# Gate products of token-tile pairs as seven quadrant products, and one ring of buffers

## The chip, the cores and the metric

The kernel runs on one core of one Trainium2 chip. The metric is the device time of a run in microseconds; the median of three runs is given. The profile is that of one execution, taken on the same core.

## The reference

One layer of a hybrid decoder for a prompt of 2048 tokens (16 tiles of 128) and a sample batch of 64 tokens. All is float32.

```
h = rms_norm(x, norm_pre); z = h @ w_in                 # 1024 -> 3584 columns
a_out = silu(sg) * spatial_gating(gelu(su), gelu(sv))   # gMLP half, chunks of 128 tokens
b_out = silu(rg) * group_norm(retention(q, k, v))       # retention half, 4 heads of 128
mix = concatenate([a_out, b_out]) @ w_out               # 1024 -> 1024
x = x + rms_norm(mix, norm_post)
x = x + sigmoid(x @ w_ple_gate) * (p @ w_ple_proj)      # gate 1024 -> 1024, embedding 256 -> 1024
```

The last line is where the change works. The gate is a product of 2048 x 1024 by 1024 x 1024, the embedding one of 2048 x 256 by 256 x 1024.

## The kernel before

Every operand of a product is split into a high part in a rounded float32 type (F32R) and a low part, the rest. A product of a token tile with a weight chunk of 128 x 512 is then three matmuls, high by high, high by low, low by high, each of 128 x 128 stationary (tokens) and 128 x 512 moving (weights). For the sample's 64 tokens the high and the low part lie side by side in one stationary operand, so two matmuls do. Making a split takes a ScalarE copy (L251 for tokens, L214 or L216 for weights) and a VectorE or GpSimd subtraction (L253, L223, L225).

The work is a list of units, one for a token tile in each of five passes: S (gMLP part of the input projection), R twice (two heads each), C1 (output projection, post norm and residual; stores the new x to DRAM as rows, `x2d`, and transposed, `x2T`) and C2 (gate and embedding, the final output). Tile order is 0 to 7, the sample, 8 to 15. A C2 unit has 24 gate matmuls for each of two groups of 512 columns, each followed by 6 matmuls of the embedding.

The class `Stream` writes out the order of all engines by hand. Its clock is a count: one main matmul issued is one count. `st.at(count, fn)` and `st.later(lag, fn)` place work at a count, generators started with `st.start` go on after the counts that they yield. The counts fix the order on each engine's queue, not the time: an engine may run ahead of TensorE as far as its operands and its buffers let it. `fill` places a weight chunk's load `LAG_W` = 14 counts ahead of its high part (L234 to L236). A unit's operands are loaded two units ahead and split one unit ahead. Loads and most stores are on SyncE's queue, in program order; C1's stores of `x2d` and `x2T` are on ScalarE's queue (L823, L826).

Buffers come from several pools: `ring`, 52 buffers of 2 KB per partition for weights; `big`, 10 of 4 KB for token operands, rows and raw loads; `t2` 10 of 2 KB, `t1` 11 of 1 KB, `v2` 8 of 2 KB and `c4` 2 of 4 KB for intermediate values. In PSUM, `zbank` gives one of 4 banks to main products and `sbank` one of 4 to side work. A tile takes any free buffer of its pool; where none is free, the instruction that first writes it waits for the release of an old one.

After a gate group ScalarE takes the tanh of half the product (L838); after the embedding group VectorE makes (tanh + 1) times the embedding (L850), adds half of it to the residual row (L853), and SyncE stores it. In C1 the chain after a unit is a sum of squares on ScalarE (L807), the scale r on GpSimd (L811, L295, L296), the scaled product on VectorE (L818), the addition to the residual on GpSimd (L822), and the block transposition (L180).

## Time and profile before

| what | value |
| --- | --- |
| median of 3 runs | 1147.72 us (1147.21 to 1148.03) |
| span of the profiled execution | 1146.2 us |
| its instructions | 15123 |
| TensorE matmuls, share of span | 5316, 99% |
| VectorE, ScalarE, GpSimd, share of span | 53%, 30%, 38% |
| moved by DMA | 157.75 MB, mean 138 GB/s |

The span runs from the first to the last instruction of one execution. The page lists no other time for that execution; the three runs lie 1.0 to 1.8 us above the span. In the profile PE is TensorE's matmuls and PEld its weight loads, DVE is VectorE, ACT ScalarE, POOL GpSimd and SP SyncE; the engine names with q are their queues. "L196" is line 196 of the kernel, where all matmuls are issued.

### The profile page before, as it was taken

To read this page: it belongs to the slowest core of one execution; us is meant where nothing else is said; L and a number is where in the kernel's file an instruction comes from. 1 tells how busy PE (TensorE), PEld (TensorE's weight loads), DVE (VectorE), ACT (ScalarE), POOL (GpSimd) and SP (SyncE) were. 2 spreads that over 40 slices of the span, in tenths; PEclk is the share of its full clock that TensorE was granted. 3 is DMA by queue.
4 is the path that set the end of the run, shared out by engine and by line. 5 is a ranking of instruction groups with operands and counts; after the bars stand their busy time and mean duration, and the time that the engine had idled before them with its cause. 6 is when DMAs were issued, how large, how long until landed. Compare 5 with 4: busy or idle time off the path is not lost.

```text
span 1146.2 us, 15123 instructions
## 1 busy us (share of the span) xinstructions
PE 1139.0 (99%) x5316; PEld 943.1 (82%) x5316; DVE 604.7 (53%) x1094; ACT 346.5 (30%) x648; POOL 436.3 (38%) x621
## 2 busy tenths in 40 slices
PE   9999999999999999999999999999999999999998
PEld 7888878888888888788888887888888888888886
DVE  4866575566745655675456457643344652233332
ACT  6543433335312322242123123412222421112110
POOL 6654434533334465653444575443334210000000
PEclk9999999999999999999999999999999999999999
DMA  9343123124353442663443427656666763335431
GB/s 312 98 146 96 40 73 119 39 85 135 101 159 96 119 110 81 189 184 97 117 121 95 117 70 213 212 193 191 202 228 227 240 221 120 108 111 150 131 106 55
DMA packets 140300, 157.75 MB, mean 138 GB/s; under 512 B 30656, under 2 KB 106688, under 8 KB 140224
## 3 DMA queue, kind: packets, MB, share of 16 engines
q1 hardware_dynamic: 128336, 139.48, 39.9%
q10 hardware_dynamic: 11888, 17.31, 4.8%
q8 instruction: 42, 0.69, 0.3%
q14 instruction: 34, 0.28, 0.1%
HBM read 110.99 MB, written 45.74 MB: 137 GB/s over the span
## 4 chain that ended last, share of the span: by engine, by line
PE 94%; DMA 2%; POOL 2%; DVE 1%; SPq 1%; issue 0%; ACT 0%; DVEq 0%; ACTq 0%; POOLq 0%
PE z L196 87%; PE s L196 7%; DMA W<-w_in 1%; DMA X<-x 1%; POOL v L377 1%; POOL t L361 0%; SPq L920 0%; DMA X<-sguT 0%; POOL X L253 0%; SPq L207 0%; DVE ti L351 0%; DVE t L337 0%; DVE t L333 0%; DVE W L225 0%; DVE X L305 0%
## 5 line engine op out<-in xcount | busy, mean ns | idle before, releaser
L196 PE MATMUL z<-W,X 128*128 128x512 f32 x4328 | 1072.6, 396 | 1.6 <-DVE W L225 0.8
L196 PEld LDWEIGHTS z<-W,X 128*128 128x128 f32 x4328 | 804.0, 188 | 164.4 <-issue 2.6
L253 DVE TENSOR_TENSOR X<-X,X 128x1024 fp32r<-128x1024 f32 (+1 forms) x68 | 81.1, 1192 | 36.6 <-PE z L196 16.4
L850 DVE SCALAR_TENSOR_TENSOR t<-t,z 128x512 f32<-128x512 f32 (+1 forms) x33 | 22.2, 672 | 142.1 <-PE z L196 142.1
L251 ACT CAST X<-X 128x1024 fp32r<-128x1024 f32 (+1 forms) x82 | 83.7, 1020 | 32.9 <-issue 22.8
L196 PEld LDWEIGHTS s<-t,t 128*128 128x128 f32 (+1 forms) x400 | 73.6, 186 | 13.1 <-issue 3.1
L196 PE MATMUL s<-t,t 128*128 128x128 f32 (+2 forms) x400 | 76.3, 272 | 0.0
L498 ACT ACTIVATE t<-z,rsall 128x256 f32<-128x256 f32 x32 | 15.2, 476 | 196.4 <-PE z L196 191.9
L180 DVE STREAM_TRANSPOSE t<-t 128x256 f32<-128x256 f32 (+3 forms) x69 | 39.8, 577 | 61.5 <-POOL t L478 42.5
L838 ACT ACTIVATE t<-z 128x512 f32<-128x512 f32 x32 | 19.1, 598 | 170.5 <-PE z L196 167.6
L474 POOL TENSOR_TENSOR t<-t,t 128x256 f32<-128x256 f32 (+1 forms) x34 | 27.3, 802 | 100.4 <-DVE t L471 86.3
L225 DVE SCALAR_TENSOR_TENSOR W<-W,c_npre,W 128x512 fp32r<-128x512 f32 x56 | 44.7, 819 | 19.9 <-ACT W L216 19.8
L822 POOL TENSOR_TENSOR X<-X,t 128x512 f32<-128x512 f32 (+1 forms) x34 | 45.7, 1364 | 18.1 <-DVE t L818 12.0
L196 PE MATMUL z<-W,t 128*128 128x512 f32 x200 | 50.9, 389 | 0.0
L535 POOL TENSOR_TENSOR ti<-ti,c_cols 128x2 f32<-128x2 f32 (+1 forms) x34 | 11.2, 328 | 96.1 <-DVE ti L531 96.1
L504 POOL TENSOR_TENSOR t<-t,gnw 128x256 f32<-128x256 f32 (+1 forms) x34 | 40.1, 1178 | 18.8 <-DVE t L502 18.4
L216 ACT ACTIVATE W<-W,c_npre 128x512 fp32r<-128x512 f32 x56 | 39.1, 719 | 25.7 <-DMA W<-w_in 23.4
L807 ACT ACTIVATE t<-z 128x512 f32<-128x512 f32 x32 | 19.1, 598 | 91.1 <-PE z L196 91.1
L196 PEld LDWEIGHTS z<-W,t 128*128 128x128 f32 x200 | 37.5, 188 | 7.8
L529 DVE BATCH_NORM_STATS2 ti<-s 128x6 f32<-128x128 f32 x64 | 15.8, 288 | 50.3 <-PE s L196 50.3
L377 POOL TENSOR_TENSOR v<-t,v 128x128 fp32r<-128x128 f32 x64 | 31.4, 512 | 23.4 <-ACT v L375 17.7
L253 POOL TENSOR_TENSOR X<-X,X 128x1024 fp32r<-128x1024 f32 (+1 forms) x14 | 32.9, 2353 | 15.7 <-ACT X L251 9.6
(118 smaller groups left out, 1042.5 us busy)
## 6 DMA issues: line engine op xcount, KB each, us to landing
X<-xT SPq DMA_DIRECT2D x45, 512.0 KB, 4.0
X<-x SPq DMA_DIRECT2D x32, 512.0 KB, 5.0
W<-w_in SPq DMA_DIRECT2D x56, 256.0 KB, 4.4
qkT<-t SPq DMA_DIRECT2D x132, 64.0 KB, 2.0
x2T<-c ACTq DMA_DIRECT2D x66, 128.0 KB, 2.6
t<-qkT SPq DMA_DIRECT2D x32, 256.0 KB, 3.0
X<-mixT SPq DMA_DIRECT2D x16, 512.0 KB, 4.4
x2d<-X ACTq DMA_DIRECT2D x16, 512.0 KB, 2.7
```

The lines of the kernel that those rows point to most:

```text
L180: V.transpose(out=out.rearrange("p b k r -> p k b r"), in_=src.rearrange("p (k b r) -> p k b r", b=4, r=32))
L196: PE.matmul(out, lhsT=l, rhs=r, start=start, stop=stop)
L216: S.activation(out=hi, in_=raw, func=AF.Copy, scale=sc)
L225: V.scalar_tensor_tensor(out=lo, in0=raw, scalar=sc, in1=f(hi), op0=ALU.mult, op1=ALU.subtract)
L251: S.copy(out=hi, in_=raw)
L253: eng.tensor_tensor(out=lo, in0=raw, in1=f(hi), op=ALU.subtract)
L377: GP.tensor_tensor(out=los[q][:, :, t % 4, :], in0=i, in1=f(o), op=ALU.subtract)
L474: GP.tensor_tensor(out=qk[:, :, 0, :], in0=t1[:, :, 0, :], in1=t2[:, :, 1, :], op=ALU.subtract)
L504: GP.tensor_tensor(out=g, in0=g, in1=ret["gn"][0:n, 256 * pr : 256 * pr + 256], op=ALU.mult)
L807: S.activation(out=junk, in_=src, func=AF.Square, accum_out=acc["a"][:, g : g + 1])
L822: GP.tensor_tensor(out=x2[:, c], in0=x2[:, c], in1=w, op=ALU.add)
L850: V.scalar_tensor_tensor(out=th[g][:, h], in0=th[g][:, h], scalar=1.0, in1=src[:, h], op0=ALU.add, op1=ALU.mult)
```

## The change

The gate is computed for two token tiles (t0, t1) together, by seven products of quadrants in place of eight (the Winograd form of Strassen's method). The two halves of the 1024 features and the two tiles form the quadrants A11 (t0, first half), A12 (t0, second half), A21 and A22 (the same of t1); the weights' quadrants are B11 to B22. GpSimd makes four sums of token quadrants (S1 to S4) and, once, four sums of weight quadrants (T1 to T4); each operand of a product is then split into high and low parts as before. The seven products go to four PSUM banks: m1, u2 and u3 are accumulated one on another in bank a, m5 and c12 in bank c, c21 and c11 have banks of their own. After m1, m5, u2 and u3 ScalarE copies the running sum to a buffer; VectorE adds such copies to the results of c12, u3, c21 and c11, which gives the four gate quadrants. The sample uses four plain quadrant products.

The embedding products of a pair stand between the quadrant products of the next pair, 6 after each of the first four; the last pair has also its own, after u3 and c21.

The pools `ring`, `big`, `v2`, `t2`, `t1` and `c4` become one ring of 101 slots of 2 KB (values of 1 KB take a slot too), with two buffers of 4 KB apart from it for C1's transposition. Tiles of 4 KB become two halves, and so their loads, splits and sums of squares come in halves, in every pass. The residual's store to `x2d` moves from ScalarE's queue to SyncE's. The gate's weights are loaded and prepared in 28 steps from 360 counts ahead of C1's last unit on. The scratch memory for descriptors is set to 1024 bytes.

```diff
+SLOTS = 101
...
-    ring = ctx.enter_context(tc.tile_pool(name="ring", bufs=52))
-    big = ctx.enter_context(tc.tile_pool(name="big", bufs=10))
+    ring = ctx.enter_context(tc.tile_pool(name="ring", bufs=SLOTS))
...
+    def slot(label, shape, dt=F32):
+
+        return ring.tile(shape, dt, tag="slot", name=name(label))
...
-    def vtile(shape, dt=F32):
-        return work.tile(shape, dt, tag="v2", name=name("v2"), bufs=8)
-
-    def xtile(shape, dt=F32):
-        return big.tile(shape, dt, tag="X", name=name("X"))
+        return slot("W", shape, dt)
...
+    def xhalves(shape, dt=F32, label="X"):
+        return [slot(label, shape, dt) for _ in range(2)]
...
     def t2k(shape, dt=F32):
-        return work.tile(shape, dt, tag="t2", name=name("t2"), bufs=10)
+        return slot("t2", shape, dt)
...
     def t1k(shape, dt=F32):
-        return work.tile(shape, dt, tag="t1", name=name("t1"), bufs=11)
...
+    PRODUCTS = {
+        "m1": ("A11", "B11", "a"), "m5": ("S1", "T1", "c"), "u2": ("S2", "T2", "a"), "c12": ("S4", "B22", "c"),
+        "u3": ("S3", "T3", "a"), "c21": ("A22", "T4", "d"), "c11": ("A12", "B21", "b"),
+    }
+    ORDER = ("m1", "m5", "u2", "c12", "u3", "c21", "c11")
+
...
+    def fast_weights(src, scale=None):
...
+        def load(r, c, k):
+            raw = slot("wraw", [P, 512])
+            SY.dma_start(out=raw, in_=src(c, 4 * r + k))
+            raws[r, c, k] = raw
...
+        def job(key, k, raw, needs=(), total=None):
...
+            def high():
+                hi = slot("W", [P, 512], F32R)
+                S.copy(out=hi, in_=raw())
+                cell.append(hi)
...
+            def low():
+                lo = slot("W", [P, 512], F32R)
+                V.tensor_tensor(out=lo, in0=raw(), in1=f(cell[0]), op=ALU.subtract)
+                table[key, k] = (cell[0], lo)
+                cell.clear()
...
+        def combine(dst, x, y, op):
+            GP.tensor_tensor(out=raws[dst], in0=raws[x], in1=raws[y], op=op)
+
+        for k in range(4):
+            job("B11", k, lambda k=k: raws[0, 0, k], [(0, 0, k)])
+        for k in range(4):
+            job("T1", k, lambda k=k: raws[0, 0, k], [(0, 1, k)],
+                lambda k=k: combine((0, 0, k), (0, 1, k), (0, 0, k), ALU.subtract))
+        for k in range(4):
+            job("T2", k, lambda k=k: raws[0, 0, k], [(1, 1, k)],
...
+        for k in range(4):
+            job("B22", k, lambda k=k: raws[1, 1, k])
...
+            job("T3", k, lambda k=k: raws[0, 1, k], [],
+                lambda k=k: combine((0, 1, k), (1, 1, k), (0, 1, k), ALU.subtract))
+        for k in range(4):
+            job("T4", k, lambda k=k: raws[0, 0, k], [(1, 0, k)],
+                lambda k=k: combine((0, 0, k), (1, 0, k), (0, 0, k), ALU.subtract))
+        for k in range(4):
+            job("B21", k, lambda k=k: raws[1, 0, k])
+        return table, jobs
...
+    def fast_fill(jobs, counts):
+        for (loads, scales, total, high, low), c in zip(jobs, counts):
+            for fn in loads:
+                st.at(c - 8 - LAG_W, fn)
+            for fn in scales:
+                st.at(c - 9, fn)
+            if total:
+                st.at(c - 7, total)
+            st.at(c, high)
+            st.at(c + 4, low)
...
+            for i, h in ((0, 0), (0, 1)) if self.sample else ((0, 0), (1, 0), (1, 1), (0, 1)):
+                t = self.tiles[i]
+                raw = slot("X", [P, np_(t) // 32, 4, 32])
+                SY.dma_start(out=raw, in_=self.source[t].rearrange("a p k r -> p a k r")[:, :, 4 * h : 4 * h + 4, :])
+                self.raw[i, h] = raw
...
+                hi, lo = ops = slot("A", [P, 4, P], F32R), slot("A", [P, 4, P], F32R)
...
+            S.copy(out=hi, in_=raw)
+            yield 4
+            V.tensor_tensor(out=lo, in0=raw, in1=f(hi), op=ALU.subtract)
+            self.ops[key] = ops
...
+        def total(self, x, y, op):
+            out = slot("sum", [P, 4, 4, 32])
+            GP.tensor_tensor(out=out, in0=x, in1=y, op=op)
+            return out
...
+            sums = {
+                "S1": lambda: self.total(r[1, 0], r[1, 1], ALU.add),
+                "S2": lambda: self.total(tot["S1"], r[0, 0], ALU.subtract),
+                "S4": lambda: self.total(r[0, 1], tot["S2"], ALU.subtract),
+                "S3": lambda: self.total(r[0, 0], r[1, 0], ALU.subtract),
+            }
+            raw = {"A11": r[0, 0], "A22": r[1, 1], "A12": r[0, 1]}
+            keys = [PRODUCTS[p][0] for p in self.order]
+            todo = [x for x in keys if x in sums]
+            for i, x in enumerate(keys):
+                if todo:
+                    y = todo.pop(0)
+                    tot[y] = sums[y]()
+                yield from self.split(x, tot[x] if x in tot else raw[x])
+                yield 8
...
+                for k in range(4):
...
+                        def go(x=x, y=y, b=b, k=k, j=j, new=new):
+                            self.need(x)
+                            start, stop = k == 0 and j == 0, k == 3 and j == 2
+                            if start and new:
+                                banks[b] = zbank() if b in "ac" else sbank()
+                            hi, lo = self.ops[x]
+                            wh, wl = self.tab[y, k]
+                            mm(banks[b], (hi, hi, lo)[j][:, k, :], (wh, wl, wh)[j], start and new, stop, not new)
+
+                        seq.append((go, None))
+                seq[-1] = (seq[-1][0], lambda p=p: st.start(self.after(p, banks)))
+                if i < len(self.aside):
+                    seq += self.aside[i]
...
+        def after(self, p, banks):
+            t0, t1 = self.tiles
+            c = self.parts = getattr(self, "parts", {})
+            yield 1
+
+            def copy(key, b):
+                c[key] = slot("C", [P, 512])
+                S.copy(out=c[key], in_=banks[b])
+
+            def add(key, b, t, part):
+                V.tensor_tensor(out=c[key], in0=banks[b], in1=c[key], op=ALU.add)
+                st.start(self.post_(t, part, c[key]), 1)
+
+            if p == "m1":
+                copy("m1", "a")
+            elif p == "m5":
+                copy("m5", "c")
+            elif p == "u2":
+                copy("u2", "a")
+            elif p == "c12":
+                add("u2", "c", t0, 1)
+            elif p == "u3":
+                copy("u3", "a")
+                add("m5", "a", t1, 1)
+            elif p == "c21":
+                add("u3", "d", t1, 0)
+            else:
+                add("m1", "b", t0, 0)
...
+        r = tiny(1)[0:n]
+        GP.tensor_tensor(out=r, in0=acc[:, 0:1], in1=acc[:, 1:2], op=ALU.add)
+        rms_scale(r, r, n, 1.0 / D)
+        yield 6
+        x2 = [h[0:n] for h in c1.pop(("tok", t))]
+        for j in range(2):
+            w = t2k([P, 512])[0:n]
+            V.scalar_tensor_tensor(
+                out=w, in0=c1.pop((j, t)), scalar=r, in1=ret["npost"][j][0:n], op0=ALU.mult, op1=ALU.mult
+            )
+            yield 3
+            GP.tensor_tensor(out=x2[j], in0=x2[j], in1=w, op=ALU.add)
+            store(x2d[t][:, 512 * j : 512 * j + 512], x2[j])
+        yield 12
+        bt = blocks(block_rows(n), x2, n)
+        scatter(x2T[t], bt, n, S)
...
+    def c2_begin(tiles):
+        def load():
+            for t in tiles:
+                for g in (1, 0):
+                    tl = slot("x2", [P, 512])[0 : np_(t)]
+                    SY.dma_start(out=tl, in_=x2d[t][:, 512 * g : 512 * g + 512])
+                    c2["x2", t, g] = tl
+
+        st.later(40 if 15 in tiles else 68, load)
...
+    def c2_post(t, g, src):
+        th = src[0 : np_(t)]
+        S.activation(out=th, in_=th, func=AF.Tanh, scale=0.5)
+        c2["th", t, g] = th
+        yield 1
...
+        yield 1
+        th, x2 = c2.pop(("th", t, g)), c2.pop(("x2", t, g))
+        w = 256 if t == 14 and g == 0 else 512
+        for o in range(0, 512, w):
+            h, c = slice(o, o + w), slice(512 * g + o, 512 * g + o + w)
+            V.scalar_tensor_tensor(out=th[:, h], in0=th[:, h], scalar=1.0, in1=ple[:, h], op0=ALU.add, op1=ALU.mult)
+            V.scalar_tensor_tensor(out=x2[:, h], in0=th[:, h], scalar=0.5, in1=x2[:, h], op0=ALU.mult, op1=ALU.add)
+            store((a["o_ys"] if t == SAMPLE else a["o_y"][t])[:, c], x2[:, h])
...
+    unitsC1 = [Unit("C", [t], tabC1) for t in order]
+    unitsC2, before = [], []
+    for j, tiles in enumerate(pairs[:4] + [[SAMPLE]] + pairs[4:]):
+        aside = [ple_products(*tg) for tg in before]
+        if tiles[0] == SAMPLE:
+            before = [(SAMPLE, 1), (SAMPLE, 0)]
+        else:
+            t0, t1 = tiles
+            before = [(t0, 1), (t1, 1), (t1, 0), (t0, 0)]
+        if j == 8:
+            own = [ple_products(*tg) for tg in before]
+            aside = (aside + [[]] * 4)[0:4] + [own[0], own[1] + own[2] + own[3]]
+        unitsC2.append(Fast(tiles, tabC2, x2T, c2_post, c2_begin, aside, c2_operands))
...
-        for steps, us in ((stepsR[1], unitsR[0]), (stepsC1, unitsR[1])):
-            fill(steps, first8(us[-3]) + [begin[us[-1]] + 6 + 6 * j for j in range(8)])
-        fill(stepsC2, [begin[unitsC1[-7]] + 40 * j for j in range(8)] + [begin[unitsC1[-1]] + c for c in (6, 12, *range(18, 66, 6), 70, 76)])
+        us = unitsR[0]
+        fill(stepsR[1], first8(us[-3]) + [begin[us[-1]] + 6 + 6 * j for j in range(8)])
+        us = unitsR[1]
+        fill(stepsC1, first8(us[-3]) + [begin[us[-1]] + 6 + 6 * j for j in range(8)])
+        last = begin[unitsC1[-1]]
+        fast_fill(jobsC2, [last - 20 * (18 - j) for j in range(18)] + [last + 8 + 9 * j for j in range(10)])
+        fill(stepsP, [last + 90 + 10 * j for j in range(4)])
...
+            if isinstance(u, Fast):
+                lead = 92, 54
...
+            st.at(begin[u] - lead[0], u.load)
+            st.at(begin[u] - lead[1], lambda u=u: start_prep(u))
...
+    nc = bacc.Bacc("TRN2", target_bir_lowering=False, num_devices=1, dynamic_dma_scratch_size=1024)
```

## Rows read from the trace of the kernel before

**Rows 1.** The page, its head and part 1: busy us of each engine.

```profile
span 1146.2 us, 15123 instructions
...
PE 1139.0 (99%) x5316; PEld 943.1 (82%) x5316; DVE 604.7 (53%) x1094; ACT 346.5 (30%) x648; POOL 436.3 (38%) x621
```

**Rows 2.** The page, part 4: chain that ended last, shares by engine.

```profile
PE 94%; DMA 2%; POOL 2%; DVE 1%; SPq 1%; issue 0%; ACT 0%; DVEq 0%; ACTq 0%; POOLq 0%
```

**Rows 3.** TensorE's waits, whole span: us in total, times, longest.

```profile
PE s L912 <- POOL zero L162: 1.0, 1, 1.0
PE z L196 <- DVE W L225: 0.8, 2, 0.5
PE z L196 <- ACT W L216: 0.5, 1, 0.5
PE z L196 <- POOL X L923: 0.3, 1, 0.3
```

**Rows 4.** Windows of C1 and C2: engines' busy us, clock, DMA share, GB/s.

```profile
734.00:914.80 180.80, 180.80 (x813) 150.13 (x811) 79.90 (x101) 49.49 (x103) 65.38 (x89) 1.00 0.65 207
914.80:1141.50 226.70, 226.70 (x1001) 187.56 (x999) 77.19 (x111) 45.23 (x77) 3.85 (x5) 1.00 0.40 129
```

**Rows 5.** Timeline of TensorE at the start of C2: start, duration.

```profile
914.80 5.60 PE L196 MATMUL z<-W,X 128*128 128x512 f32 x24
920.24 1.52 PE L196 MATMUL z<-W,t 128*128 128x512 f32 x6
921.60 5.60 PE L196 MATMUL z<-W,X 128*128 128x512 f32 x24
...
928.40 5.60 PE L196 MATMUL z<-W,X 128*128 128x512 f32 x24
```

**Rows 6.** Timeline of all engines at the end.

```profile
1140.11 1.52 PE L196 MATMUL z<-W,t 128*128 128x512 f32 x6
1140.30 0.60 ACT L838 ACTIVATE t<-z 128x512 f32<-128x512 f32 x1 [6.20 <-PE z L196]
1141.73 0.42 DVE L850 SCALAR_TENSOR_TENSOR t<-t,z 128x256 f32<-128x256 f32 x1 [5.38 <-PE z L196]
...
1142.98 0.42 DVE L853 SCALAR_TENSOR_TENSOR X<-t,X 128x256 f32<-128x256 f32 x1
```

**Rows 7.** Groups of instructions in C2: busy us, mean ns, idle before.

```profile
L850 DVE SCALAR_TENSOR_TENSOR t<-t,z 128x512 f32<-128x512 f32 x31 | 21.3, 689 | 136.7 <-PE z L196 136.7
L838 ACT ACTIVATE t<-z 128x512 f32<-128x512 f32 x32 | 19.1, 598 | 170.5 <-PE z L196 167.6 <-DMA x2T<-c 2.9
...
L223 DVE TENSOR_TENSOR W<-W,W 128x512 fp32r<-128x512 f32 x6 | 4.1, 680 | 2.3 <-ACT W L214 2.3
```

**Rows 8.** Timeline of all engines after a unit of C1.

```profile
860.59 0.38 SPq L720 DMA_DIRECT2D X<-mixT  x1
860.60 0.60 ACT L807 ACTIVATE t<-z 128x512 f32<-128x512 f32 x1 [1.68 <-PE z L196]
...
863.48 2.99 POOL L822 TENSOR_TENSOR X<-X,t 128x512 f32<-128x512 f32 x2 [0.87 <-DVE t L818]
...
866.51 1.25 DVE L180 STREAM_TRANSPOSE c<-X 128x1024 f32<-128x1024 f32 x1 [1.18 <-POOL X L822]
```

**Rows 9.** Groups of VectorE, ScalarE and GpSimd in C1, asked by engine.

```profile
L223 DVE TENSOR_TENSOR W<-W,W 128x512 fp32r<-128x512 f32 x12 | 11.0, 923 | 1.7 <-ACT W L214 1.7
...
L214 ACT CAST W<-W 128x512 fp32r<-128x512 f32 x13 | 7.8, 616 | 4.1 <-DMA W<-w_gate 1.8 <-POOL X L822 1.7 <-PE z L196 0.6
...
L822 POOL TENSOR_TENSOR X<-X,t 128x512 f32<-128x512 f32 x30 | 39.8, 1348 | 14.8 <-DVE t L818 9.6 <-issue 5.2
```

**Rows 10.** DMA issues in C1: count, KB each, median us to landing.

```profile
X<-mixT SPq DMA_DIRECT2D x12, 512.0 KB, 4.3
W<-w_gate SPq DMA_DIRECT2D x16, 256.0 KB, 4.3
```

**Rows 11.** Waits of SyncE's queue in C1: us in total, times, longest.

```profile
SPq L720 <- PE z L196: 74.8, 11, 10.1
```

More of the change, by code (lines that the diff above doesn't have):

```diff
@@ new lines, in hybrid_step, with c2_operands @@
+    c2 = {}
+    def c2_begin(tiles):
[6 more added lines that the diff above has]
+        st.later(40 if 15 in tiles else 68, load)
+    def c2_operands(tiles):
+        raws = []
+        for t in tiles:
+            raw = t1k([P, 2, P])[:, :, 0 : np_(t)]
+            SY.dma_start(out=raw, in_=(a["psT"] if t == SAMPLE else a["pT"][t]))
+            raws.append(raw)
+        yield 14
+        for t, raw in zip(tiles, raws):
+            z = slot("A", [P, 2, 2, P], F32R)
+            if t == SAMPLE:
+                hi, lo, ops = z[:, 0, :, 0:TS], z[:, 0, :, TS:P], (z[:, 0],)
+            else:
+                hi, lo = ops = z[:, 0], z[:, 1]
+            S.copy(out=hi, in_=raw)
+            yield 3
+            V.tensor_tensor(out=lo, in0=raw, in1=f(hi), op=ALU.subtract)
+            yield 3
+            c2["p", t] = ops
@@ new lines, in load @@
+                if self.kind == "C":
+                    self.raw[t] = xhalves([P, np_(t) // 32, 4, 32])
+                    for h in range(2):
+                        src = mixT[t].rearrange("a p k r -> p a k r")[:, :, 4 * h : 4 * h + 4, :]
+                        SY.dma_start(out=self.raw[t][h], in_=src)
+                    continue
+                self.raw[t] = load_xT(t)
+                if self.kind == "R":
+                    if t == SAMPLE:
+                        st.start(r_sample_state(self.pr))
+                    cs = work.tile([P, P], F32, tag="cs", name=name("cs"), bufs=3)
+                    SY.dma_start(out=cs[0 : np_(t)], in_=a["cs"][t, 0 : np_(t)])
+                    ret["cs", t] = cs
+                else:
+                    self.raw["tok", t] = load_tok(t)
@@ L752, in begin @@
-        def begin(self):
-            t = self.tiles[0]
-            if self.kind == "C1":
-                self.raw["tok", t] = load_tok(t)
-            elif self.kind == "C2":
-                x2 = xtile([P, D])[0 : np_(t)]
-                SY.dma_start(out=x2, in_=x2d[t])
-                self.raw["x2", t] = x2
+                self.ops[t] = yield from split_cols(self.raw.pop(t), t, GP if self.kind == "S" else V)
+                if self.kind == "S":
+                    yield 2
+                    yield from rms_of_x(t, self.raw["tok", t])
+                    if t == SAMPLE:
+                        st.start(sgu_weights_sample())
@@ L761, in main, with load @@
+        def begin(self):
+            if self.kind == "C":
+                t = self.tiles[0]
+                def load():
+                    c1["tok", t] = load_tok(t)
+                st.later(20, load)
         def main(self):
@@ L791, in main @@
                                 seq += p[3 * k : 3 * k + 3]
-            elif kind == "R":
+            elif kind == "C":
+                t = self.tiles[0]
+                for g in range(2):
+                    seq += group(t, opsof(t), g, range(KD), lambda b, g=g: c1_post(t, g, b))
+            else:
                 t, pr = self.tiles[0], self.pr
@@ L870, in hybrid_step @@
     order = list(range(8)) + [SAMPLE] + list(range(8, NT))
+    pairs = [[2 * j, 2 * j + 1] for j in range(NT // 2)]
     tabS, fillS = weight_pass(in_specs([1, 0, 2]))
```

407 lines of the change are left out of this document (223 added, 184 removed).

## The prediction, made before the changed kernel ran

> **What bounds the kernel now.** I read the page from the top. TensorE is busy for 1139.0 of 1146.2 us [rows 1] and the chain that ended last lies on it for 94% of the span [rows 2]. Busy alone proves little, so the next view is TensorE's own waits: apart from 1.0 us at the very start there are 1.6 us of them in all [rows 3]. Then I cut the span at the change. In the output-projection pass (C1) and the gate pass (C2) the granted clock is 1.00, the 2.4 GHz level, TensorE never stands, VectorE is busy for 80 of 181 and 77 of 227 us, ScalarE for 49 and 45, GpSimd for 65 and 4, and the DMA engines are at 65% and 40% [rows 4]. Last comes the spacing. In C2 a period of 24 gate products and 6 embedding products begins at 914.80 us and the next but one at 928.40: 60 products in 13.60 us, 226.7 ns each, whichever kind they are [rows 5]. C2 has 16 x 60 + 40 = 1000; 1000 x 0.2267 = 226.7 us, from 914.80 to about 1141.5. So C2 costs its count of products times one step, and a product less is worth 0.2267 us for as long as TensorE is still fed.
>
> **What is removed.** A pair of token tiles takes 2 x 48 = 96 gate products now. Seven quadrant products of 4 k-blocks and 3 hi/lo terms are 84. The sample stays at 32 and the embedding at 200. The new C2 has 8 x 84 + 32 + 200 = 904, which is 96 fewer: 96 x 0.2267 = 21.8 us. Shapes are unchanged, so I keep the step. The Trainium skill (TensorE: Matmul & The Clock Gate, "Wait — 56ns, not 53.3ns?") measures 215.7 ns from one product of 512 columns to the next at the full clock; by that page the 96 would bring 20.7 us, an estimate, and the row of this kernel is 5% longer.
>
> **What is added at the end.** Today TensorE ends on embedding products. The tanh of their gate ran beside them (1140.30), and four VectorE instructions of 0.42 us follow from 1141.73 [rows 6]. After the change the product c11 comes last. Behind it stand a VectorE add out of PSUM (priced like L850, 0.69), a tanh (L838, 0.60) [rows 7], two hand-overs between engines, and then the same four instructions. A hand-over took 0.04 us (866.47 to 866.51) [rows 8]; I take 0.1 each. The end grows by 0.69 + 0.60 + 0.2 = 1.5 us; the bounds are 0, if the stores get shorter by as much, and 2.
>
> **What is added beside TensorE in C2.** A full pair is 84 + 24 products, 24.5 us. ScalarE: 7 casts and 4 copies at 0.62, 4 tanh at 0.60, 9.2 us. VectorE: 7 low parts at 0.68 (L223 with GpSimd idle) to 0.92 (with GpSimd at work), 4 adds and 8 instructions of the tail's kind at 0.69 (L850): 13.0 to 14.7 us. GpSimd: 4 sums at 1.35 (L822), 5.4 us [rows 7, 9]. The embedding's own splits are as now. At most 60% of a pair is taken, and all of it is hidden behind 24.5 us of products; without that cover VectorE's 14.7 us would be what a pair costs.
>
> **A new wait.** Banks a and c are read in the middle of a sum: u2 goes on in bank a only when m1 is copied out, c12 in bank c when m5 is, u3 in bank a when u2 is. From the last product of one to the next write of its bank lie 24 products where the embedding stands between (5.4 us), 12 in the first pair, which has none (2.7 us). The copy takes 0.6, so ScalarE may come 4.8 us late, or 2.1 in the first pair, before TensorE stands. In front of it are casts that wait for loads or sums. Quadrants are loaded 92 - 54 = 38 counts (8.6 us) ahead of their first cast and land in some 4.3 us [rows 10]; a sum is asked for a whole product ahead. In the first pair there are also weight steps of T4 and B21: from load to combination 15 counts, 3.4 us, against 4.3 to land, so 0.9 late; the combination takes 1.35 of the 1.6 us that it has; the cast, and what is queued behind it, comes 0.7 us late. That is under 2.1. I take 0; from above three waits of 2 us, 6 us.
>
> **In C1.** Eighteen weight steps stand ahead of the last unit where 8 were: 10 x 0.62 us more on ScalarE, 10 x 0.92 on VectorE and some ten combinations x 1.35 on GpSimd [rows 9], over 181 us with room for each [rows 4]. A unit's two banks are read for the last time some 62 counts after its first product and wanted again at 96, so the chain L807, r, L818 may slip by 34 counts, 7.7 us; a combination and a late cast in front of it are 2 to 3 us. SyncE issues about 7 loads and stores per unit for 3, at 0.38 us each [rows 8], 2.7 of 10.9 us. The residual's two stores move to it from ScalarE's queue, and operand and weight loads stand behind them. They wait for L822, whose second sum ends 5.9 us (26 counts) after its unit's products [rows 8], and are placed 27 and 30 counts after: they hold the queue for little. Loads in halves shorten the runs of the transposed operands. If those 8.4 MB per pass took twice the time, the DMA share would go from 65% to 79% in C1 and from 40% of 227 us to 57% of 205 in C2, worked out from the rates in [rows 4]: still hidden. S and R keep their products; a lag in their added halves would have to use up a whole unit (5 us and more) to show.
>
> **The ring.** One ring of 101 slots serves what five kinds of buffer did. By the lags in the diff, C2 holds 64 slots of weights, up to 12 of operands, 5 quadrants, 2 sums, 5 partial products, 6 residual halves and 4 embedding operands; they do not peak together, and I count 94 at most. Tightest is the point 28 counts ahead of C1's last unit: 32 + 34 weights, 10 raw chunks, 4 quadrants, 8 operands, 8 others, 96. Five are to spare. Today's kernel shows what a full pool does: SyncE stood 74.8 us in all for buffers that TensorE was still reading, up to 10.1 at a time [rows 11], and TensorE waited for none of it [rows 3].
>
> **Sum.** -21.8 + 1.5 = -20.3 us on a span of 1146.2: 1125.9. The median of the runs, 1147.72, stands 1.5 us above that span. Forecast: 1127.5 us, itself between 1124.8 (no growth at the end and 1 of the 1.6 us of early waits gone, as early loads no longer wait for large buffers: 1147.7 - 21.8 - 1.0 = 1124.9) and 1129 (1.5 us of the first pair's bound).
>
> **Rivals.**
> A, stalls at the edges: the first pair's copies, or C1's banks behind late combinations, hold TensorE for 2 to 8 us. For it: only 2.1 us of room, and weight steps that come late already. Against: loads and casts are queued ahead of TensorE and run when they can, not when their count comes. 1129.5 to 1135.5 us. Chance 0.22.
> B, slower: each copy of a partial product needs a fresh slot. If the ring is dry in the steady state, ScalarE stands at the copy until an older slot is free, and TensorE stands with it, three times in each of 8 pairs. That eats the gain when each bank is 20.3 / 24 = 0.85 us late, the copy done 6.3 us behind its product instead of within 5.4. At 2 us each the time is 1127.5 + 48 = 1175. For it: some seven slots to spare by my count in C2. Against: with a slot freed every few products a wait would be short. Chance 0.07, and 0.03 that it stops within 2.3 us of the old time.
> C, C2 does not shorten with its products: the weight loads are busy for 82% of the span [rows 1], and if that were the measure, TensorE would not be the limit. The 226.7 us would stay and the end would grow: 1149. Against: no wait in C2, and a period that repeats to 0.01 us. Chance 0.02. The Trainium skill (Trainium Kernel Development and Optimization, "Performance Expectations") calls matmul busy time a bad metric and weight-load busy a good one; this trace bears it out only as far as that 82%.
>
> **How the numbers follow.** Forecast 0.66, A 0.22, B 0.07 + 0.03, C 0.02. Faster by over 0.2% (2.3 us, about what a measurement of this kernel can tell from no change): 0.66 + 0.22 = 0.88. Within it: 0.03 + 0.02 = 0.05. Slower: 0.07. The range, 1124.8 to 1135.5, takes in the forecast and A.
>
> **What would show it.** Right: C2 in 205 us, still 226.7 ns a product, TensorE waiting for no copy; the last store issued some 1.5 us later after the last product than now. Wrong: TensorE standing at the start of u2, c12 or u3; ScalarE standing at a copy or cast for an old slot; a clock below the 2.4 GHz level in C2; another step; a C1 longer than 181 us.

## The result, and the profile of the changed kernel

The changed kernel takes 1132.4 us (median of four runs: 1131.08, 1133.74, 1130.59, 1133.72), the kernel before 1147.87 on the same chip. The ratio is 0.9865, with an interval of 0.9851 to 0.9879: faster by 15.5 us, inside the predicted range and 4.9 us above the forecast. The profiled execution is the run of 1131.08; its span is 1129.3.

The page, part 1, against [rows 1]:

```profile
PE 1118.1 (99%) x5220; PEld 925.4 (82%) x5220; DVE 687.1 (61%) x1283; ACT 395.7 (35%) x834; POOL 504.8 (45%) x700
```

96 products fewer and TensorE's share as before. VectorE has 82 us more work, GpSimd 69, ScalarE 49. The page can't say where a few us are missing; TensorE's waits over the whole span can, against [rows 3]:

```profile
PE z L202 <- ACT C L907: 1.4, 1, 1.4
PE s L202 <- DVE W L229: 1.4, 2, 0.9
PE s L1209 <- POOL zero L163: 1.0, 1, 1.0
PE s L202 <- ACT W L220: 0.4, 1, 0.4
```

L907 is the copy of a partial product, L220 and L229 are the high and low parts of the embedding's weights. These three waits are new. The same view has three more, 0.9 us in all, ahead of C1. The timeline of TensorE puts them at two places, the start of u2 in the first pair and the first six embedding products that stand in the second pair:

```profile
912.68 6.51 PE L202 MATMUL z<-W,A 128*128 128x512 f32 x28
920.63 8.46 PE L202 MATMUL z<-W,A 128*128 128x512 f32 x36 [1.45 <-ACT C L907]
928.93 5.60 PE L202 MATMUL s<-W,A 128*128 128x512 f32 x24
934.37 2.88 PE L202 MATMUL z<-W,A 128*128 128x512 f32 x12
937.35 0.50 PE L202 MATMUL s<-W,A 128*128 128x512 f32 x1
938.35 0.73 PE L202 MATMUL s<-W,A 128*128 128x512 f32 x2 [0.51 <-DVE W L229]
939.44 0.50 PE L202 MATMUL s<-W,A 128*128 128x512 f32 x1 [0.36 <-ACT W L220]
940.85 0.73 PE L202 MATMUL s<-W,A 128*128 128x512 f32 x2 [0.91 <-DVE W L229]
```

From 934.37, 18 products should take 4.1 us; the next group of 12 begins at 941.42, 7.05 later. So 3.0 us go here. That is more than the 1.8 that the waits hold, because a product that stands alone takes 0.50 us in these rows and not the step of 0.2267. Another 1.6 go at 920.63 (28 products from 912.68 should end their steps at 919.03), together 4.6. After that nothing is lost. A later pair in the same view:

```profile
961.84 2.88 PE L202 MATMUL z<-W,A 128*128 128x512 f32 x12
...
986.32 0.84 PE L202 MATMUL z<-W,A 128*128 128x512 f32 x3
```

From 961.84 to 986.32 are 24.48 us for 108 products, 226.7 ns each, as in [rows 5]. What the other engines do at the two places is seen by windows (busy us of each engine, granted clock, DMA share, GB/s), the first the whole of C1, against [rows 4]:

```profile
734.00:913.70 179.70, 179.70 (x806) 149.13 (x805) 93.22 (x136) 55.37 (x126) 91.44 (x106) 1.00 0.67 208
```

and the change from C1 to C2 in steps of 10 us:

```profile
895.00:905.00 10.00, 10.00 (x46) 8.28 (x45) 5.81 (x8) 3.54 (x8) 9.14 (x9) 1.00 0.66 192
905.00:915.00 10.00, 10.00 (x46) 8.29 (x45) 6.40 (x8) 3.60 (x7) 10.00 (x8) 1.00 0.64 215
915.00:925.00 10.00, 8.55 (x38) 6.78 (x37) 10.00 (x11) 7.74 (x15) 8.89 (x9) 1.00 0.54 150
925.00:935.00 10.00, 10.00 (x46) 8.29 (x45) 9.93 (x12) 2.33 (x5) 6.75 (x5) 1.00 0.86 277
```

The columns after the length are TensorE's products, its weight loads, VectorE, ScalarE, GpSimd. GpSimd is half busy over C1 (91 of 180 us) and all but full at its end (9.14 and 10.0 of 10 us); then VectorE is full for 20 us. How the one leads to the other shows in the timeline of these two and ScalarE:

```profile
907.80 1.74 POOL L835 TENSOR_TENSOR sum<-X,sum 128x512 f32<-128x512 f32 x1
908.31 1.78 DVE L830 TENSOR_TENSOR A<-sum,A 128x512 fp32r<-128x512 f32 x1
909.50 1.73 POOL L994 TENSOR_TENSOR X<-X,t 128x512 f32<-128x512 f32 x1
911.19 2.54 POOL L765 TENSOR_TENSOR wraw<-wraw,wraw 128x512 f32<-128x512 f32 x2
912.51 0.62 ACT L753 CAST W<-wraw 128x512 fp32r<-128x512 f32 x1 [3.48 <-POOL wraw L765]
913.16 1.12 DVE L758 TENSOR_TENSOR W<-wraw,W 128x512 fp32r<-128x512 f32 x1 [3.08 <-ACT W L753]
...
915.94 0.62 ACT L828 CAST A<-sum 128x512 fp32r<-128x512 f32 x1 [1.55 <-DVE bt L184]
...
920.00 0.58 ACT L907 COPY C<-z 128x512 f32<-128x512 f32 x1
...
934.63 0.63 ACT L1035 ACTIVATE C<-C 128x512 f32<-128x512 f32 x1 [4.28 <-DVE C L910]
935.17 0.60 ACT L220 CAST W<-W 128x512 fp32r<-128x512 f32 x1
```

ScalarE stands 3.48 us at a weight cast for a weight sum (L765), which stands behind a token sum (L835) and a residual add (L994) on GpSimd. VectorE stands behind that cast, 3.08 us. When both go on, VectorE is late with some ten subtractions, and many of them are long: up to 1.78 us beside a GpSimd sum, against 0.69 on average for the same instruction in four later pairs. The copy at 920.00 waits for nothing when its turn comes. It is late because ScalarE's queue ahead of it stood for the weight sum and then another 1.55 us, at a store that waits for VectorE's transposition. The second stall comes the same way: the casts of the embedding's weights (L220) stand behind a tanh that waits 4.28 us for an add of VectorE (L910).

The end, in the timeline of all engines, against [rows 6]; the last product ends at about 1123.4 and the span at 1129.3, 5.9 us after it, where it was 4.6 (1141.6 and 1146.2):

```profile
1120.73 2.65 PE L202 MATMUL s<-W,A 128*128 128x512 f32 x11
...
1123.43 0.69 DVE L910 TENSOR_TENSOR C<-s,C 128x512 f32<-128x512 f32 x1 [2.60 <-PE s L202]
1124.15 0.63 ACT L1035 ACTIVATE C<-C 128x512 f32<-128x512 f32 x1 [6.17 <-DVE C L910]
1124.81 0.42 DVE L1049 SCALAR_TENSOR_TENSOR C<-C,s 128x256 f32<-128x256 f32 x1 [0.69 <-ACT C L1035]
```

The group of 28 at 912.68 holds C1's last 4 products, so C2 starts at 913.6, 1.2 us earlier than in [rows 4]. The account of the span: -21.8 for the products, -1.2 for the start, +4.6 for the two stalls, +1.3 for the end, -17.1; measured 1146.2 - 1129.3 = 16.9.

### The profile page after: what moved, and what is told of

Its sections match the earlier page's. It is cut to its first block, busy times and chain, and to the rows that moved or that the text cites. A ratio compares the mean times of both kernels' runs of the same rounds, so it can differ in the third digit from the quotient of the medians.

```text
span 1129.3 us, 15843 instructions
## 1 busy us (share of the span) xinstructions
PE 1118.1 (99%) x5220; PEld 925.4 (82%) x5220; DVE 687.1 (61%) x1283; ACT 395.7 (35%) x834; POOL 504.8 (45%) x700
## 4 chain that ended last, share of the span: by engine, by line
PE 95%; DVE 1%; POOL 1%; issue 1%; DMA 1%; ACT 0%; SPq 0%; DVEq 0%; ACTq 0%; POOLq 0%
PE z L202 80%; PE s L202 16%; POOL wraw L765 1%; DVE W L758 0%; DVE A L830 0%; DMA t<-xT 0%; POOL sum L835 0%; POOL X L994 0%; DVE C L910 0%; DMA wraw<-w_gate 0%; DVE W L229 0%; ACT A L828 0%; POOL A L1221 0%; ACT C L1035 0%; DVE x L1050 0%
## 5 line engine op out<-in xcount | busy, mean ns | idle before, releaser
L202 PE MATMUL z<-W,A 128*128 128x512 f32 x4040 | 1007.5, 396 | 2.4 <-ACT C L907 1.4
L202 PEld LDWEIGHTS z<-W,A 128*128 128x128 f32 x4040 | 750.1, 188 | 153.3 <-issue 2.6
L202 PE MATMUL s<-W,A 128*128 128x512 f32 x464 | 112.5, 390 | 1.9 <-DVE W L229 1.4
L202 PEld LDWEIGHTS s<-W,A 128*128 128x128 f32 x464 | 86.9, 188 | 21.2 <-DVE W L229 2.0
L262 DVE TENSOR_TENSOR A<-X,A 128x512 fp32r<-128x512 f32 (+1 forms) x102 | 73.4, 722 | 46.1 <-ACT A L260 39.3
L260 ACT CAST A<-X 128x512 fp32r<-128x512 f32 (+1 forms) x130 | 78.2, 603 | 22.8 <-issue 14.6
L835 POOL TENSOR_TENSOR sum<-X,X 128x512 f32<-128x512 f32 x16 | 23.1, 1445 | 93.1 <-DMA X<-x2T 44.8
L994 POOL TENSOR_TENSOR X<-X,t 128x512 f32<-128x512 f32 (+1 forms) x34 | 46.3, 1382 | 14.0 <-DVE t L990 13.0
L1035 ACT ACTIVATE C<-C 128x512 f32<-128x512 f32 (+1 forms) x34 | 21.5, 632 | 63.2 <-DVE C L910 60.9
L262 POOL TENSOR_TENSOR A<-X,A 128x512 fp32r<-128x512 f32 (+1 forms) x28 | 35.5, 1273 | 14.3 <-ACT A L260 14.3
L347 ACT ACTIVATE t<-z,rsall 128x512 f32<-128x512 f32 x29 | 19.8, 687 | 60.9 <-PE z L202 60.8
```

Source lines behind the costliest of these rows:

```text
L202: PE.matmul(out, lhsT=l, rhs=r, start=start, stop=stop, skip_group_check=again)
L260: S.copy(out=hi, in_=r)
L262: eng.tensor_tensor(out=lo, in0=r, in1=f(hi), op=ALU.subtract)
L347: S.activation(out=g, in_=src, func=AF.Square, scale=rs)
L835: GP.tensor_tensor(out=out, in0=x, in1=y, op=op)
L994: GP.tensor_tensor(out=x2[j], in0=x2[j], in1=w, op=ALU.add)
```

## The experiments

The main question was where 4.6 us of the gain went, and why; the rest tests the prediction's other terms. Unless said otherwise an edit is made to the changed kernel, and its time is to be held against 1132.4 and 0.9865 [0.9851, 0.9879].

**The embedding products of the first pair later.** They stand after c12, u3, c21 and c11 of the second pair, and no longer after its first four products.

```diff
+        if j == 1:
+            aside = [[], [], []] + aside
         unitsC2.append(Fast(tiles, tabC2, x2T, c2_post, c2_begin, aside, c2_operands))
```

> The embedding products of the first pair, which stand in the second pair, are moved three products later (after c12, u3, c21 and c11 instead of m1, m5, u2 and c12). Theory 1, VectorE has a backlog of some 10 us at the change from C1 to C2 and the embedding's weight parts stand in it: the broken stretch of 6 embedding products (937.1 to 941.4 us, 3.0 us longer than six steps) is whole again, the span falls by 2.7 to 3.0 us, to about 1126.4, and the runs that showed a granted clock of 0.997 or 0.998 instead of 0.999 no longer do, so that the median falls by more, to 1128. Rival, all that VectorE makes is late: the wait moves to the operands of m5, u2 or c12 of the second pair and the time stays within 0.5 us of the changed kernel's.

1135.49 us, 0.9892 [0.9879, 0.9906], 3 us slower. TensorE's waits:

```profile
PE z L202 <- ACT C L907: 5.9, 2, 4.4
```

and its timeline at the second pair:

```profile
939.82 0.39 PE L202 MATMUL z<-W,A 128*128 128x512 f32 x1
944.64 7.36 PE L202 MATMUL z<-W,A 128*128 128x512 f32 x24 [4.43 <-ACT C L907]
```

The wait for embedding weights is gone and a larger one for the copy stands in front of u2 of the second pair. So it is not those weights alone that are late, but what ScalarE and VectorE make as a whole. The edit has two other effects. The embedding products are also the 6 x 0.2267 us of room that a copy has, and here that room is gone. And the granted clock falls behind the longer stall: the 24 products take 7.36 us, for 5.60 at the 2.4 GHz level, so 1.8 us of what this execution loses are the clock.

**The end covered.** The last pair's second half of embedding products is put behind c11.

```diff
-            aside = (aside + [[]] * 4)[0:4] + [own[0], own[1] + own[2] + own[3]]
+            aside = (aside + [[]] * 4)[0:4] + [own[0], own[1] + own[2], own[3]]
```

> Of the last pair's own embedding products the last six stand behind c11, not before it. Theory 1 (the end grew because an add of 0.69 and a tanh of 0.63 us stand behind the last product): those 1.4 us run beside six products of 1.36 us, and the span falls by 1.2 to 1.3 us. Rival, the end grew for another reason, its stores or queues: no change.

1130.92 us, 0.9857 [0.9843, 0.9870]. The timeline at the end: c11's add runs beside six products that end at about 1125.0, the span ends at 1129.5, 4.5 later, where it was 4.6 before the change.

```profile
1119.81 5.15 PE L202 MATMUL s<-W,A 128*128 128x512 f32 x22
...
1123.64 0.69 DVE L910 TENSOR_TENSOR C<-s,C 128x512 f32<-128x512 f32 x1 [1.23 <-PE s L202]
```

The 1.3 us at the end are shown by the trace; the intervals of the two times overlap, so the time alone would not show them. Nor does the span, 1129.5 for 1129.3: in this execution the granted clock fell after the second stall (0.83 in 935 to 945 us), which it did not in the changed kernel's.

**No weight sums.** GpSimd's sums T1 to T4 are left out, so the gate is computed with the plain weight chunks in their place; everything else runs.

```diff
-            if total:
-                st.at(c - 7, total)
```

> GpSimd's 16 subtractions that make T1 to T4 are left out, so the gate is computed from the plain quadrants and its values are not the reference's. All other instructions stay. Theory 1 as a question of speed, GpSimd at work on SBUF stretches VectorE's subtractions: the low parts of the gate's weights fall from 1.08 us on average to below 0.8, the backlog shrinks, and of the 4.6 us that TensorE loses in the first two pairs at least 3 come back: a span of 1126.3 or less. Rival, the sheer number of VectorE's instructions there makes the backlog: the low parts may get faster but TensorE still loses 3.5 us or more. Second rival, slots of the ring: no change, as no slot is freed earlier.

1127.15 us, 0.9821 [0.9808, 0.9835], 5.2 us faster, and the four runs lie within 0.3 us. The profiled executions, in neither of which the clock fell in C2, lie 4.1 us apart (1125.2 and 1129.3), which is the stalls; the rest goes with the clock, told below. Of TensorE's waits in C2 one is left:

```profile
PE s L202 <- DVE W L229: 0.4, 1, 0.4
```

and the window shows GpSimd with time to spare:

```profile
905.00:915.00 10.00, 10.00 (x46) 8.29 (x45) 9.56 (x12) 4.41 (x10) 7.27 (x5) 1.00 0.60 206
```

GpSimd's weight sums are what the stalls hang on. VectorE does more of its work ahead of C2 (9.56 of 10 us in 905 to 915, for 6.40). That its subtractions would then get short was a miss: L758 still takes 987 ns on average over the pass, for 1078, and between 895 and 941 us, where the stalls were, nearly as long as before:

```profile
L758 DVE TENSOR_TENSOR W<-wraw,W 128x512 fp32r<-128x512 f32 x11 | 13.4, 1225 | 0.4 <-ACT W L753 0.3
```

**The ring alone.** The ring, the halves and the queues of the new kernel with the old gate, tile by tile, in it.

```diff
-    unitsC2, before = [], []
...
+    unitsC2 = [Unit("G", [t], tabC2) for t in order]
```

> The one ring and the halves stay, but the gate is computed as before, tile by tile with 96 products a pair, its embedding behind each group, 20 weight steps at their old places. Theory: the ring brings the 1.2 us by which R and C2 begin earlier, and nothing else: 1146.7 us, TensorE's waits after the start under 1.5 us. Rival 1, halves and the shared ring cost something in S, R or C1 that the earlier start hides: above 1147.9. Rival 2, the earlier start comes from the changed order of loads near C2 and not from the ring: 1147.9.

1146.96 us (11 runs) for 1147.58 of before (15 runs), 0.9995 [0.9986, 1.0004]. The medians lie 0.6 us apart and the interval reaches from 1.6 us less to 0.5 more, so no cost and no gain of the ring with its halves is shown. Its C1 waits for nothing and C2 begins at 914.2.

**Sums that nobody reads.** GpSimd makes the weight sums into a buffer of their own and the casts take the plain chunks, so the gate's values differ as above: its work stays, the waiting of the casts for it goes.

```diff
-            GP.tensor_tensor(out=raws[dst], in0=raws[x], in1=raws[y], op=op)
+            GP.tensor_tensor(out=slot("unused", [P, 512]), in0=raws[x], in1=raws[y], op=op)
```

> GpSimd makes its 16 weight sums at the same places and speed, but into buffers that nobody reads; T1 to T4 are the plain quadrants, so the gate's values are not the reference's. This separates two ways in which leaving the sums out took 4 us off. Theory A, the casts of T1 to T4 on ScalarE wait for late sums, hold ScalarE's queue and let VectorE's work pile up behind: without the wait the pile is gone, 1127 to 1128 us, TensorE losing under 1 us in the first two pairs. Theory B, GpSimd at work stretches VectorE's instructions and its own residual additions come late behind the sums: the load is the same, so the time stays at 1131 us or more.

1134.53 us, 0.9887 [0.9872, 0.9902], no gain at all; TensorE's three waits in C2 come to 4.6 us, for 3.2. The buffers of the unused sums take slots of the ring, but GpSimd waits for none of them, only for loads. My first theory, that the casts wait for weight sums and hold up what is behind them, falls in this form. The timeline of ScalarE shows what takes their place:

```profile
917.70 0.62 ACT L828 CAST A<-sum 128x512 fp32r<-128x512 f32 x1 [5.74 <-POOL sum L835]
```

The token sums of the first pair stand in the same queue on GpSimd. It is GpSimd's load in this stretch that counts, whoever waits for it first. Whether it counts by its lateness or by what it does to VectorE's subtractions, this run can't tell: both are still there.

**Weights k-block by k-block.** All seven steps of a k-block follow each other, 21 of 28 before C1's last unit, so that sums and plain steps alternate.

```diff
         for k in range(4):
             job("B11", k, lambda k=k: raws[0, 0, k], [(0, 0, k)])
-        for k in range(4):
             job("T1", k, lambda k=k: raws[0, 0, k], [(0, 1, k)],
...
-        for k in range(4):
...
-        fast_fill(jobsC2, [last - 20 * (18 - j) for j in range(18)] + [last + 8 + 9 * j for j in range(10)])
+        fast_fill(jobsC2, [last - 20 * (21 - j) for j in range(21)] + [last + 13 * j for j in range(7)])
```

> The 28 weight steps come k-block by k-block: all seven operands of k = 0, 1 and 2 ahead of C1's last unit, 20 counts apart, and the seven of k = 3 in the order of their products, 13 counts apart, from that unit's start. Raw chunks are free after their k-block, so the ring has room for 21 early steps where there were 18. Seven weight sums of GpSimd between 897 and 919 us become four or five. Theory (GpSimd, fully busy from 895 to 921 us, is what holds the others): TensorE's lost 4.6 us fall below 1.5, the granted clock is 0.999 in all runs, 1127.5 to 1129 us. Rival, VectorE's amount of work at the edge: 3 low parts fewer are 2 to 3 us of its backlog of 10, the loss stays above 3 us, 1130 or more.

1130.91 us, 0.9855 [0.9841, 0.9868], where I had expected 1127.5 to 1129. TensorE waits 2.4 us for a copy and 0.9 for L229, 3.3 together, for 3.2 in the changed kernel. The profiled executions have the same span, 1129.3, so no stall is mended: the median is 1.5 us lower because no run is as long as the two at 1133.7, and the intervals overlap. Of ScalarE's waits between 890 and 945 us one is new in size:

```profile
ACT W L753 <- PE z L202: 3.0, 1, 3.0
```

GpSimd has gaps now (4.45 of 10 us in 895 to 905), but ScalarE stands 3.0 us for a slot of the ring that TensorE still reads, and 8.5 us for weight sums, more than the 6.3 of the changed kernel. Earlier steps need slots that aren't there at that moment.

**Ninety slots.** `SLOTS = 90` for 101.

> The changed kernel with 90 slots in the ring for 101. Theory, the ring is no cause of what TensorE loses: by the count of the prediction up to 96 are in use at one place, so loads there come some counts later, but the time stays within 1 us of the changed kernel's 1130.6 to 1133.7. Rival (the prediction's B): the ring is nearly dry already, and eleven slots less cost 5 us or more, with TensorE waiting at banks a and c in many pairs.

1139.8 us, 0.9932 [0.9920, 0.9945]; I had expected less than 1 us, and it is 7.4. Waits of TensorE in the whole span:

```profile
PE z L202 <- ACT C L907: 8.0, 1, 8.0
PE z L202 <- DVE t L990: 2.0, 1, 2.0
```

Between 890 and 945 us ScalarE stands 11.7 us for slots that TensorE still reads and 9.9 for weight sums. The ring is short at the change from C1 to C2 and nowhere else: the steady pairs show no wait. The 8 us are one wait, in the first pair. Behind it the granted clock is 0.52 in 925 to 935 us, so a part of the 7.4 is the clock.

**Both edits together**, the weights by k-block and the covered end:

> The weight steps by k-block together with the last six embedding products behind c11. If both causes are what the theory says, their gains add: 1.2 us less than the run with the weight steps alone, 1126.3 to 1127.8 us. Rival: the end's gain is taken by something else, and the two runs are equal.

1129.8 us, 0.9846 [0.9833, 0.9859], 1.1 less than the first alone, near the 1.2 expected, though the intervals overlap and the time is above the 1126.3 to 1127.8 expected. By its median it is the fastest version that computes the whole layer, 1.5% under the kernel before.

**103 slots.** `SLOTS = 103`.

> The ring has 103 slots for 101, nothing else. With 101 slots the trace of the changed kernel shows one wait of ScalarE for a slot that TensorE still reads, 1.9 us. Theory (the stalls come from GpSimd's full stretch; 101 slots are enough): 1131.5 to 1133, and TensorE's idle before the copy of L907 stays at 1.2 to 1.6 us, that before the embedding weights at about 1.8. Rival (the ring at 101 still holds the casts up, a milder form of what 90 slots did): the wait for the slot is gone and the time falls by 1 to 3 us, to 1129 to 1131.

1133.14 us, 0.9875 [0.9858, 0.9891]. ScalarE's wait for a slot is gone, TensorE waits 2.6 us for the copy, for 1.45, and 0.9 for the embedding's weights, for 1.8; the time is no better. At 101 the ring is not what binds.

**Six sums on VectorE.** Meant were the last six weight sums; the condition as written fits two others, of T1, some 20 of the 28 steps before the last.

```diff
-            GP.tensor_tensor(out=raws[dst], in0=raws[x], in1=raws[y], op=op)
+            late = y[0:2] == (1, 0) or (x[0:2] == (0, 1) and y[2] > 1)
+            (V if late else GP).tensor_tensor(out=raws[dst], in0=raws[x], in1=raws[y], op=op)
```

> The last six weight sums (T3 from its third k-block, T4) go to VectorE, the other sums stay on GpSimd. GpSimd is relieved of 6 sums of about 1.3 us in 900 to 925 us, VectorE gets 6 of about 0.7 us, 4 us, while it is busy for 6.4 of 10 us in 905 to 915 and without a gap after that. Theory (GpSimd's queue is what is late; token sums stand behind weight sums): the wait for the copy of L907 goes from 1.45 to under 0.5, and the time to 1128 to 1130. Rival (VectorE is as full as GpSimd from 915 us on, so that the work only changes its place): the wait moves to the embedding weights' low parts of L229 and grows there to 3 us or more; 1131 to 1134.

1132.3 us, 0.9865 [0.9850, 0.9880]: as without the edit. It says nothing on the question; moving the late sums to VectorE was not tried. Its trace is of use below, as the changed kernel's own with another clock.

**The transposed tile's stores on SyncE.**

```diff
-        scatter(x2T[t], bt, n, S)
+        scatter(x2T[t], bt, n, SY)
```

> The four stores of each transposed token tile (x2T) are issued from SyncE and not from ScalarE, in all 17 units of C1. ScalarE no longer waits for the transposition of L184 (1.55 us at 915.94 in the changed kernel's trace) with the copies of m1 and m5 behind it. Theory (the first copy is late because of what stands ahead of it on ScalarE, the sums of GpSimd and this store): half of it goes, the wait of 1.45 falls to under 0.6, time 1130.5 to 1132. Rival (the cast ahead of it is late from GpSimd's sums alone, and SyncE's queue now holds quadrant and weight loads behind the transposition): no gain, 1132 to 1136.

1132.73 us, 0.9868 [0.9854, 0.9883], no gain; TensorE waits 2.6 us for the copy, for 1.45. ScalarE no longer waits for the transposition and waits 10.3 us for weight sums in place of 6.3: the rival. With another wait taken out of ScalarE's queue, GpSimd's lateness is what is left.

**T3 before B22, and the covered end.** The steps with four sums change places with four that have none, T4 and B21 come later.

```diff
+        if scale is None:
+            jobs[12:20] = jobs[16:20] + jobs[12:16]
         return table, jobs
...
-        fast_fill(jobsC2, [last - 20 * (18 - j) for j in range(18)] + [last + 8 + 9 * j for j in range(10)])
+        fast_fill(jobsC2, [last - 20 * (18 - j) for j in range(18)] + [last + 8, last + 17] + [last + 36 + 7 * j for j in range(8)])
```

> The order of the gate weights' steps: T3 (which needs four sums of GpSimd) is made before B22 (which needs none), the T4 and B21 steps start 10 counts later and follow each other by 7 and not by 9; the last six embedding products stand after c11, as in the run with the covered end, whose time was 1130.9. Nothing is added or taken away. Theory (what is late at the start of the gate pass is GpSimd, which four weight sums of T3, 5.8 us, fill up between 895 and 921 us together with the first pair's token sums and C1's residual adds): GpSimd is busy for under 9 of 10 us in 905 to 915, ScalarE no longer stands at a weight cast there, the wait of 1.45 us before the copy of L907 falls under 0.5, and the time comes to 1127.5 to 1129.5. Rival (VectorE, busy without a gap from 915 to 935, is what is late, and it has as many low parts to make as before): the waits for L229 and L220 stay at 1.5 us or more, 1130 to 1132.

1130.92 us, 0.9856 [0.9839, 0.9872], the same as the covered end alone. Of the theory a part came: in 905 to 915 us VectorE is busy for 9.28 us, for 6.40, but GpSimd still for 9.06, and ScalarE stands for weight sums 5.8 us, for 6.3; TensorE waits 1.0 for the copy, for 1.45. TensorE waits longer for the embedding's weights than before, 2.4 us for 1.8, which is the rival: VectorE has the same subtractions to make, still beside GpSimd.

## Why the prediction was right, and where it was off

**What bounds the kernel, what is removed.** Right, and exact: 226.7 ns a product after 941.4 us, for gate and embedding alike. Rival C is out. The Trainium skill (TensorE: Matmul & The Clock Gate, "Wait — 56ns, not 53.3ns?") has 215.7 ns from one product of 512 columns to the next at the full clock, by which the 96 would be worth 20.7 us, an estimate; the pair of 108 products in 24.48 us, 226.7 ns each, does not agree with it.

**The end.** +1.5 forecast, +1.3 measured: add 0.69, tanh 0.63, hand-overs of under 0.1 us. Covering it takes it back.

**The early start.** It stood in the lower bound alone. C2 began 1.2 us earlier in the profiled execution, and 0.6 earlier in that of the run with the old gate. Of the 1.6 us of early waits that this bound was made from, 0.9 are left in the first and 0.3 in the second, so the start does not follow them; what brings it is open, and it can't be told from scatter between executions.

**A new wait.** Right in place, wrong in price. The prediction put the first pair's copies at 2.1 us of room and what is late at 0.7 us, and took 0; the first copy came 1.5 us too late for TensorE. TensorE stands at the start of u2, one of the prediction's own signs of being wrong. The embedding weights, another 3.0 us, were "as now", and were not thought of.

**In C1: the step that failed.** "Some ten combinations x 1.35 on GpSimd, over 181 us with room for each". The count and the price are near (L765 took 1.38 us on average, 1.44 in 895 to 941 us), the averaging over 181 us is what was wrong. Seven of the weight sums, the first pair's token sums and C1's last residual adds fall into 895 to 921 us, and there GpSimd has no room: 9.14 and 10.0 of 10 us. Leaving out the weight sums takes the time to 1127.15, level with the forecast of 1127.5. The same lines of the prediction priced VectorE's low part at 0.92; it takes 1.29 on average where it matters. The group of its weight low parts in 895 to 941 us:

```profile
L758 DVE TENSOR_TENSOR W<-wraw,W 128x512 fp32r<-128x512 f32 x11 | 14.1, 1293 | 5.6 <-ACT W L753 5.6
```

and the same subtraction for token operands in four later pairs (961.84 to 1059.8 us):

```profile
L830 DVE TENSOR_TENSOR A<-sum,A 128x512 fp32r<-128x512 f32 x13 | 8.8, 686 | 7.2 <-ACT A L828 7.2
```

11 x (1.29 - 0.69) = 6.6 us of a stretch in which VectorE has no gap from 915 to 935. What stays open is the split between the two: how much of the 4.6 us is GpSimd's lateness and how much is VectorE's slowness beside it. The run without weight sums removes the first and little of the second: there the same 11 take 1.23 each, so that 5.9 of the 6.6 us stay, and yet 4.1 of the 4.6 come back. So this slowness alone does not make the stalls; what it adds to the lateness is not shown. The run with T3 earlier removes little of the lateness (ScalarE stands 5.8 us for weight sums, for 6.3) and keeps the stall of the embedding weights, so it does not separate the two.

**The ring.** The place named was right: 11 slots fewer cost 7.4 us there, two more bring nothing. The count of five to spare is not shown: at 101 slots ScalarE already stands 1.9 us for a slot that TensorE still reads. Rival B needed a dry ring in the steady pairs; even with 90 slots TensorE stands for no copy there.

**Rival A** is nearest to what happened: 4.6 us at the edges, within its 2 to 8. But only 1.6 of them stand where it put them, at the first pair's copies; 3.0 stand at the embedding's weights, which it does not name, so that its size fits is in part luck. The early start takes 1.2 us off again. The forecast held by its range, not by its likeliest case. By the account above the profiled run stands at 1147.9 - 16.9 = 1131.0; the median is 1.4 us higher, which goes with the clock, told below; the prediction has that as a sign of being wrong, and in no term.

## What to carry to other kernels

An engine that is half idle over a pass can be full in the last part of it. Where a change brings work forward into the end of a stage, cut that view at the scale of the deadline (here 10 us, not 181) and add up what all stages put there on each engine, GpSimd first, since everything behind a late sum waits in order on ScalarE and VectorE. Here the term that removes products was exact, and all that was given back, apart from the clock, lay at the handover between stages and at the end.

## What the runs showed of the hardware

**VectorE beside GpSimd.** A subtraction of VectorE with two SBUF inputs takes 0.68 us alone and up to 1.78 beside a sum of GpSimd. In the rows above one starts at 908.31, GpSimd's sum ends at 909.54, and the subtraction ends at 910.09, 0.55 after it. The Trainium skill (SBUF — State Buffer, "Who interferes with whom") says that a VectorE instruction with two SBUF inputs contends with a GpSimd instruction that reads SBUF, and that the one that issues second waits until the first is done. These rows agree: it looks like a wait for the other's end and then most of the normal duration. GpSimd's own sum takes 1.74 there and 1.28 at its shortest.

**The clock after a short stall.** In the changed kernel's profile the granted clock stays at the 2.4 GHz level after the stall of 935 to 941 us:

```profile
935.00:945.00 10.00, 8.13 (x32) 5.64 (x32) 6.77 (x10) 6.74 (x14) 1.83 (x2) 1.00 0.58 170
```

In the run with two T1 sums moved, whose TensorE waits are the same to 0.1 us, it does not. TensorE's timeline there:

```profile
941.19 1.22 PE L202 MATMUL s<-W,A 128*128 128x512 f32 x2 [0.92 <-DVE W L229]
942.21 3.93 PE L202 MATMUL z<-W,A 128*128 128x512 f32 x12
945.98 1.52 PE L202 MATMUL s<-W,A 128*128 128x512 f32 x6
```

and the window of 10 us, whose mean clock of 0.83 lies between the two levels, 1.2 and 2.4 GHz:

```profile
935.00:945.00 10.00, 8.13 (x26) 5.54 (x25) 6.71 (x12) 7.36 (x14) 1.45 (x1) 0.83 0.67 198
```

The 14 products from 941.19 take 4.79 us to the next group, for 3.31 in the changed kernel (940.85 to 944.16): 1.5 us for one stall, on top of it. The two runs at 1133.7 have a mean clock of 0.997 and 0.998, the two at 1130.6 and 1131.1 have 0.999. The kernel before and the one without weight sums, which have no such stall, keep 0.998 to 1.0, and their runs lie within 2.1 and 0.3 us. So a stall of a few us can cost twice, the second time not in every run; why in some was not settled. The 1.5 us of the row also do not cover all of the 2.6 to 3.2 us between the two pairs of runs; the longer two were not traced.
